# One block of a gated DeltaNet and attention model on one core: x transposed on arrival, adaLN weights in pieces of two K tiles, and the q and k projections of head 1 moved into the first stage

## The chip, the core and the metric

The program runs on one core of a Trainium2 chip. The metric is the device time of one execution in microseconds (us). A core has five engines that run side by side, each with an instruction stream of its own: TensorE (PE in the profile, with its weight loads as PEld), VectorE (DVE), ScalarE (ACT), GpSimd (POOL) and SyncE (SP), which in this program issues the DMAs. SBUF is the core's memory of 128 partitions, PSUM the eight banks into which TensorE writes.

## The reference

512 latent tokens and 256 context tokens of 2048 channels pass through one layer. All inputs are float32.

```python
mod = silu(c) @ w_ada + b_ada            # shift, scale, gate
h  = rms_norm(x, norm_w) * (1 + scale) + shift
hc = rms_norm(ctx, norm_w) * (1 + scale_c) + shift_c
p  = h @ w_in                            # q, k, v, z of 8 DeltaNet heads, gates, q, k, v, z of attention
# group A: centred conv of 5 taps and silu on q, k, v; chunks of 64;
#          delta-rule scan in both directions per head, over context and latents
# group B: 8 query heads on 2 k/v heads, rms-normed q and k, rope,
#          softmax over context and latents
y  = concat([norm(o_gdn) * silu(z_g), attn * silu(z_a)]) @ w_out
out = rms_norm(x + gate * y, final_norm_w)
```

## The kernel before, in words

The contraction over the 2048 channels runs in KT = 16 K tiles of 128. Activations lie transposed in SBUF, channels on partitions. A product of h with a weight is made in three passes: the high part of the weight with the high part of h, the high part with the low part, and the low part with the high part (`whi`, `wlo`, `hh`, `hl`; `hhL` and `hlL` hold the 512 latents, `hhC` and `hlC` the 256 context tokens). So one block of 128 weight columns is, for each K tile, three matmuls of 512 columns and, where the context is wanted too, three of 256.

**First stage (L220 to L331).** SP first loads small vectors. `ada(k)` (L245) computes shift and scale of K tile k: four pieces `wada` of 128 x 4 x 2 x 128 (each two DMAs of 256 KB in rows of 512 bytes, L253, four buffers), sixteen matmuls into four column groups of one bank (L255), a copy `part` on DVE (L258), two transposes `adat` (L261) and three small DVE operations into `md`. It runs two K tiles ahead. x and ctx are loaded into one tile `xs` by six DMAs of 1 MB in rows of 8 KB (L274), which stand in SP's queue behind the pieces of `ada(0)`. For each of the six the squares are summed on ACT (L282), the power -0.5 taken on POOL (L209), and the tile is scaled on DVE (L287). Then the loop over K tiles (L298): six transposes `xt` (L306), `hf` = `xt` times scale plus shift on DVE (L308), the high part on ACT (L311), the low part on DVE (L312), the gate columns `gps` (L315), 384 weight columns `wraw` (L321) split by ACT (L322) and POOL (L323), and the products k, v and q of head 0: `klat`, `vlat`, `qlat` with 512 columns (L327) and `cctx` with 256 for k and v (L330). In this stage a scheduler sets the order of every engine.

**Behind it** TensorE's order is the program order (`manual_schedule`, L897). `gdn_post_k`, `_q` and `_v` convolve a projected head: ACT copies PSUM into one of two buffers `craw`, DVE does four taps for k and v in two parts (L199, eight instructions) or for q in one (four). `gates(0, 1)` and `gates(1, NH)` make the decay factors, `gdn_prep(h)` the matrices of head h (its first matmul on TensorE that needs DVE is `tvh`, L620), and `gdn_scan(h)` runs the twelve dependent steps of head h: `ksh` (L717), `rh` on DVE (L731), `tsh` (L740), `vsh` on ACT (L744), `tsh` (L751), `sth` on DVE (L757). Between these dependent pieces stands filler: `feeding()` is one long list of projections (of the next heads, of attention's q, k, v and of the attention gate z), and `pull(n)` puts the next n matmul columns of that list into TensorE's order. Each scan step pulls 3900 + 2700 + 3200 columns (`F1`, `F2`, `F3`). A scan begins only when the next head is fully fed; the last one, of head 7, is run beside the preparation of attention (`attn_prep`). When the list is used up, `pull` adds nothing. The end of a head's scan shows in the trace as its last transposes `oth` (L778). Behind the last scan come attention, the z projections (L1197) and the output product (L139 to L141).

Of the kernel before, what the change touches and what calls it, by code (L numbers as in the profile page):

```python
# [68 lines left out]
def build(tc, a):  # L69
# [18 lines left out]
    hlL = hp.tile([128, KT, SEQ], F32R, name="hlL")  # L88
# [58 lines left out]
    def proj_steps(col, nm, pl, pc=None):  # L147


        for kq in range(4):  # L150
            src = w_in[kq * 512:(kq + 1) * 512, col:col + 128].rearrange("(k p) c -> p k c", p=128)
            hi, lo = wpiece(src, f"{nm}_{kq}", 128)
            for k4 in range(4):
                k = kq * 4 + k4
                for lw, rt, st, sp in ((hi[:, k4], hh, k == 0, False), (hi[:, k4], hl, False, False),
                                       (lo[:, k4], hh, False, k == KT - 1)):
                    T.matmul(pl, lhsT=lw, rhs=rt[0][:, k], start=st, stop=sp, skip_group_check=True)  # L157
                    if pc is not None:
                        T.matmul(pc, lhsT=lw, rhs=rt[1][:, k], start=st, stop=sp, skip_group_check=True)  # L159
# [1253 lines left out]
```

## Time and profile before

| | us |
|---|---|
| median of 3 runs | 1400.63 |
| lowest and highest | 1399.64 and 1403.52 |
| the profiled execution, span | 1401.1 |

For the profiled execution only the span is given; it lies inside the range of the runs. The profile has these kinds of rows. The page gives the busy time of each engine and its share, then the span in 40 slices of 35 us with a digit for the busy share, the granted clock of TensorE (`PEclk`) and the DMA rate. The timeline gives for each instruction, or run of like instructions, its start, its duration, engine, source line, result and operands, and in brackets the idle time of the engine ahead of it with what ended it. The waits view sums such idle time by engine, line and releaser. The windows view gives for a stretch the busy time of PE, PEld, DVE, ACT and POOL, then the granted clock, the share of the DMA engines and GB/s. An fp32 matmul stands in the trace as two instructions, so that its count is twice that of the program.

### The profile page before, as it was taken

How to read it: one execution, taken by the hardware profiler on the slowest of the kernel's cores; microseconds unless marked ns; L12 is line 12 of the kernel's file. 1: busy time of each engine (PE TensorE's matmuls, PEld its weight loads, DVE VectorE, ACT ScalarE, POOL GpSimd, SP SyncE). 2: the span in 40 equal slices, each digit the busy share in tenths (PEclk: the TensorE clock that was granted, in tenths of full speed). 3: DMA queues.
4: the chain of work that ended last, by engine and by line, in shares of the span. 5: the costliest groups of instructions: out<-in, count | busy, mean ns of one | idle time of the engine just before them, and what ended most of it. 6: DMA issues, size and time to landing. Idle time of an engine off the chain costs nothing.

```text
span 1401.1 us, 24994 instructions
## 1 busy us (share of the span) xinstructions
PE 1277.1 (91%) x9406; PEld 1023.1 (73%) x9406; DVE 755.5 (54%) x1650; ACT 609.2 (43%) x1509; POOL 520.5 (37%) x470
## 2 busy tenths in 40 slices
PE   3888898999999999999999999889999999999997
PEld 1455576877888787787777887767777787777785
DVE  3444685566546656476665624427676665544322
ACT  4111342445444453544545444446566664433221
POOL 1011211334253453443434444534777772011330
PEclk9999998999999999999999999999999999999998
DMA  9999632222323223232232344353545432474302
GB/s 312 280 286 282 162 71 61 59 63 57 74 66 74 62 69 73 58 83 57 82 61 65 71 121 122 90 189 99 162 137 158 133 102 59 169 231 143 94 33 100
DMA packets 264187, 163.52 MB, mean 117 GB/s; under 512 B 63042, under 2 KB 236187, under 8 KB 263043
## 3 DMA queue, kind: packets, MB, share of 16 engines
q1 hardware_dynamic: 264067, 161.93, 42.1%
q8 instruction: 74, 1.21, 0.4%
q14 instruction: 46, 0.38, 0.1%
HBM read 148.33 MB, written 13.56 MB: 116 GB/s over the span
## 4 chain that ended last, share of the span: by engine, by line
PE 53%; DVE 18%; issue 8%; DMA 8%; ACT 7%; POOL 4%; SPq 2%; POOLq 0%; ACTq 0%; DVEq 0%
PE vl L157 5%; PE zl L1197 5%; PE kl L157 3%; PE vx L159 3%; DVE cacc_v L199 2%; DVE cacc_k L199 2%; PE kvl L157 2%; DMA wada<-in_w_ada 2%; PE tsh L751 2%; PE ql L157 2%; PE po L140 2%; PE po L141 2%; PE po L139 2%; PE tsh L740 2%; PE ada L255 2%
## 5 line engine op out<-in xcount | busy, mean ns | idle before, releaser
L215 POOL TENSOR_TENSOR sdh<-sth,egl 128x256 f32<-128x256 f32 x80 | 55.5, 694 | 169.7 <-DVE sth L757 75.7
L1238 POOL TENSOR_TENSOR gacc<-graw,gacc 128x512 f32<-128x512 f32 x60 | 90.1, 1502 | 48.3 <-ACT graw L1236 35.8
L736 ACT ACTIVATE oqh<-ksh,egsw 64x128 f32<-64x128 f32 x128 | 46.4, 362 | 99.2 <-DVE rh L731 98.4
L123 POOL TENSOR_TENSOR wlo_z<-wraw_z,whi_z 128x512 fp32r<-128x512 f32 x52 | 69.7, 1342 | 52.4 <-ACT whi_z L122 52.4
L731 DVE SCALAR_TENSOR_TENSOR rh<-ksh,negeg,vtokh 64x128 f32<-64x128 f32 x176 | 61.2, 348 | 50.8 <-PE ksh L719 47.5
L1197 PE MATMUL zl<-hhL,whi_z 128*128 128x512 f32 x208 | 85.4, 411 | 0.0
L1197 PE MATMUL zl<-hhL,wlo_z 128*128 128x512 f32 x208 | 82.5, 397 | 0.1
L1197 PE MATMUL zl<-hlL,whi_z 128*128 128x512 f32 x208 | 82.5, 397 | 0.0
L757 DVE TENSOR_TENSOR sth<-sdh,tsh 128x256 f32<-128x256 f32 x80 | 33.7, 421 | 87.2 <-PE tsh L751 81.9
L140 PE MATMUL po<-wlo_wo,mh 128*128 128x512 f32 x192 | 76.8, 400 | 4.0 <-DVE wlo_wo L123 4.0
L139 PE MATMUL po<-whi_wo,mh 128*128 128x512 f32 x192 | 76.1, 399 | 3.1 <-DVE tt L215 1.6
L141 PE MATMUL po<-whi_wo,ml 128*128 128x512 f32 x192 | 76.0, 396 | 0.0
L123 DVE TENSOR_TENSOR wlo_wo<-wraw_wo,whi_wo 128x512 fp32r<-128x512 f32 x48 | 37.7, 794 | 65.7 <-ACT whi_wo L122 65.7
L199 DVE SCALAR_TENSOR_TENSOR cacc_v<-craw,cvT,cacc_v 128x512 f32<-128x512 f32 (+1 forms) x64 | 44.0, 734 | 38.9 <-ACT cacc_v L195 38.5
L1344 POOL TENSOR_TENSOR yx<-yx,tt 128x512 f32<-128x512 f32 x12 | 17.2, 1447 | 128.0 <-DVE tt L215 67.6
L816 DVE TENSOR_TENSOR ptl<-pt,pth 128x512 fp32r<-128x512 f32 x48 | 31.9, 688 | 58.4 <-ACT pth L815 58.2
L751 PE MATMUL tsh<-vsh,ktok 128*128 128x128 f32 x352 | 55.6, 281 | 3.6 <-ACT vsh L744 3.2
L122 ACT CAST whi_wo<-wraw_wo 128x512 fp32r<-128x512 f32 x48 | 29.2, 618 | 60.6 <-PE po L141 40.8
L323 POOL TENSOR_TENSOR wlo<-wraw,whi 128x384 fp32r<-128x384 f32 x16 | 16.1, 1013 | 106.1 <-ACT whi L322 106.1
L751 PEld LDWEIGHTS tsh<-vsh,ktok 128*128 128x128 f32 x352 | 47.8, 192 | 10.1 <-ACT vsh L744 4.6
L744 ACT ACTIVATE vsh<-tsh,cch 128x128 f32<-128x128 f32 x88 | 32.3, 367 | 45.7 <-PE tsh L740 44.7
L1119 ACT ACTIVATE pr<-s,mx 128x768 f32<-128x768 f32 x32 | 28.6, 898 | 53.2 <-PE zl L1197 32.7
(488 smaller groups left out, 4165.2 us busy)
## 6 DMA issues: line engine op xcount, KB each, us to landing
wada<-in_w_ada SPq DMA_DIRECT2D x128, 256.0 KB, 5.3
graw<-in_w_ada SPq DMA_DIRECT2D x64, 256.0 KB, 2.6
wraw_z<-in_w_in SPq DMA_DIRECT2D x52, 256.0 KB, 3.2
wraw_wo<-in_w_out SPq DMA_DIRECT2D x48, 256.0 KB, 3.5
wraw_q<-in_w_in SPq DMA_DIRECT2D x28, 256.0 KB, 3.1
wraw_k<-in_w_in SPq DMA_DIRECT2D x28, 256.0 KB, 2.8
wraw_v<-in_w_in SPq DMA_DIRECT2D x28, 256.0 KB, 2.8
xs<-in_x SPq DMA_DIRECT2D x4, 1024.0 KB
```

The source lines that it names most:

```text
L123: (lo_eng or G).tensor_tensor(out=lo, in0=raw, in1=hi, op=ALU.subtract)
L139: T.matmul(out, lhsT=lh, rhs=rh, start=start, stop=False, skip_group_check=True)
L140: T.matmul(out, lhsT=lh, rhs=rl, start=False, stop=False, skip_group_check=True)
L141: T.matmul(out, lhsT=ll, rhs=rh, start=False, stop=stop, skip_group_check=True)
L157: T.matmul(pl, lhsT=lw, rhs=rt[0][:, k], start=st, stop=sp, skip_group_check=True)
L199: V.scalar_tensor_tensor(out=x, in0=raw[:, i0 + j:i0 + j + m], scalar=w(j), in1=x, op0=ALU.mult, op1=ALU.add)
L215: eng.tensor_tensor(out=out, in0=x, in1=y, op=ALU.mult)
L731: V.scalar_tensor_tensor(out=r[rows], in0=ks[rows, d], scalar=gsc["negeg"][rows, gcol:gcol + 1], in1=vtok[rows, p], op0=ALU.mult, op1=ALU.add)
L736: S.activation(oq[rows, v, p - 2], ks[rows, d], AF.Copy, scale=gsc["egsw"][rows, gcol:gcol + 1])
L751: T.matmul(ts[:, d], lhsT=ktok[:, p, half], rhs=vs, start=True, stop=True, skip_group_check=True)
L1197: T.matmul(pl, lhsT=lw, rhs=rt[:, k], start=st, stop=sp, skip_group_check=True)
L1238: G.tensor_tensor(out=acc, in0=raw, in1=acc, op=ALU.add)
```

## The change

Seven things change together.

1. x and ctx come first in SP's queue, each of the six in a tile of its own. The pool `big` has five buffers of 8 KB per partition, which the x tiles and the `wada` pieces share. Each x tile is squared, scaled and transposed at once: sixteen transposes in ten groups, over four PSUM banks, whose copies into SBUF go in turn to DVE and ACT. The copies lie where the low part of h is written later.
2. K tiles come in groups of 1, 1, 2, 2, 2, 2, 2, 2, 1, 1. For a pair, `ada` loads four pieces of 128 x 4 x 2 x 256 (rows of 1 KB, 512 KB for each DMA) and multiplies 512 columns at once; for a single tile two pieces of 128 x 8 x 2 x 128 in rows of 512 bytes.
3. `first_weights` loads 640 weight columns for a K tile: q and k of heads 0 and 1 in rows of 1 KB, v of head 0 in rows of 512 bytes. `project(k)` makes five column blocks: `klat0`, `vlat0`, `klat1`, `qlat0`, `qlat1`.
4. TensorE's order is written out from the x transposes on: one piece of `ada(g + 2)` behind each column block, `gps` at the end of a K tile.
5. Behind the stage, `gdn_post_k(1)` and `gdn_post_q(1)` follow those of head 0, with three buffers `craw` in place of two.
6. The list of filler loses q and k of head 1 (24,576 and 36,864 columns, 61,440 together) and is ordered anew: v of head 1, the four k and v blocks of attention, then for each head h from 2 on k, q, v and the attention query block h - 2.
7. Some pulls grow: 16000 to 22000, 12000 and 4000 to 14000 and 6000, 3000 to 8000, and the last five of `prep` from 41000 together to 53000.

```diff
+    GROUPS = (1, 1, 2, 2, 2, 2, 2, 2, 1, 1)
...
+    es_p0.enter_context(tc.manual_schedule(engines={mybir.EngineType.PE}))
+    BIG = 5
...
+        for g, n in enumerate(GROUPS):
+            tp = banks[(t * len(GROUPS) + g) % 4](f"xt{t}_{g}")[:, :n]
...
+                T.transpose(out=tp[:, i], in_=xt_[:, c0:c0 + 128], identity=ident)
...
+            if g % 2:
+                S.copy(dst, tp)
+            else:
+                V.tensor_copy(dst, tp)
...
+        cols, rows = n * 128, 4 if n == 2 else 8
...
+                SY.dma_start(wt[:, :, s], src.rearrange("(k p) c -> p k c", p=128))
...
+                T.matmul(ada_ps[32 * q:32 * q + 32, :2 * cols], lhsT=cs[:, kk], rhs=wt[:, r].rearrange("p s c -> p (s c)"),
...
+        for c, pl, pcx in ((2, klat, cctx[:, 0]), (4, vlat, cctx[:, 1]), (3, klat1, cctx1[:, 0]),
+                           (0, qlat, None), (1, qlat1, None)):
...
+            yield
...
+    for g in range(len(GROUPS)):
+        if g + 1 < len(GROUPS):
+            group_h(g + 1)
+        ahead = ada(g + 2) if g + 2 < len(GROUPS) else iter(())
+        for i in range(GROUPS[g]):
+            for _ in project(first_k[g] + i):
+                next(ahead, None)
...
-    craw = [cvp.tile([128, 774], F32, name=f"craw{i}") for i in range(2)]
+    craw = [cvp.tile([128, 774], F32, name=f"craw{i}") for i in range(3)]
...
+    gdn_post_k(1, klat1, cctx1[:, 0])
+    gdn_post_q(1, qlat1)
...
-        yield from feed_q(1)
-        yield from feed_k(1)
         yield from feed_v(1)
-        yield from feed_kva(0)
+        for i in range(4):
+            yield from feed_kva(i)
+        fed.add("kva")
         for h in range(2, NH):
             yield from feed_k(h)
             yield from feed_q(h)
             yield from feed_v(h)
-            yield from feed_kva(h - 1) if h < 4 else feed_qa(h - 4)
-        yield from feed_kva(3)
-        fed.add("kva")
-        for h in range(4, NH):
+            yield from feed_qa(h - 2)
+        for h in range(6, NH):
             yield from feed_qa(h)
...
-    pull(16000)
+    pull(22000)
...
-    for n in (3000, 5500, 5500, 4000, 12000, 4000):
+    for n in (3000, 5500, 5500, 4000, 14000, 6000):
...
-    run(g1, 3000, 9000, 3000)
+    run(g1, 3000, 9000, 8000)
...
-    run(prep, 4000, 24000, 4000, 5000, 4000)
+    run(prep, 5000, 30000, 5000, 7000, 6000)
```

**TensorE in the first stage.** Before, around one K tile; `ada_501` belongs to a K tile two further on, and the projection of this K tile starts at `klat`:

```order
L306 MATMUL xt_0_694<-cmain,xs 128x128 x4
L306 MATMUL xt_1_700<-cmain,xs 128x128 x2
L255 MATMUL ada_501<-wada_12_523,cs 32x256 x4
L261 MATMUL adat_532<-cmain,part_530 128x128 x2
L327 MATMUL klat_265<-hhL,whi_3_558 128x512
L330 MATMUL cctx_268<-hhC,whi_3_558 128x256
L327 MATMUL klat_265<-hlL,whi_3_558 128x512
L330 MATMUL cctx_268<-hlC,whi_3_558 128x256
L327 MATMUL klat_265<-hhL,wlo_3_559 128x512
```

In the change, at its first K tile (`klat_512` is k of head 0, `vlat_513` v of head 0):

```order
L383 MATMUL klat_512<-hhL,w0h_464 128x512
L385 MATMUL cctx_517<-hhC,w0h_464 128x256
L383 MATMUL klat_512<-hL_475,w0h_464 128x512
L385 MATMUL cctx_517<-hC_476,w0h_464 128x256
L383 MATMUL klat_512<-hhL,w0l_465 128x512
L385 MATMUL cctx_517<-hhC,w0l_465 128x256
L319 MATMUL ada_541<-wada_0_542,cs 32x512 x4
L383 MATMUL vlat_513<-hhL,w0h_464 128x512
L385 MATMUL cctx_517<-hhC,w0h_464 128x256
```

The transposes of x have left the K tile, and a piece of `ada`, now 512 columns wide, stands between two column blocks instead of ahead of all of them.

**TensorE in the last scan, of head 7.** Before, from the eleventh step on, with z blocks of attention (`zal1a`, `zal2a`) as filler:

```order
L717 MATMUL ksh_9229<-sth_9_9836,kq_7804 128x128
L719 MATMUL ksh_9229<-sth_9_9836,kq_7804 128x128
L157 MATMUL zal1a<-hlL,whi_z1a_9808 128x512
L157 MATMUL zal1a<-hhL,wlo_z1a_9809 128x512
L157 MATMUL zal2a<-hhL,whi_z2a_9861 128x512
L157 MATMUL zal2a<-hlL,whi_z2a_9861 128x512
L157 MATMUL zal2a<-hhL,wlo_z2a_9862 128x512
...
L820 MATMUL qtp_9871<-cmain,ktok_1555 128x128 x4
L740 MATMUL tsh_10_9880<-rh_10_9845,UU_2029 128x128
```

In the change, from the fifth step into the sixth (`ktp` and `kps` belong to the preparation of attention):

```order
L827 MATMUL tsh_4_9597<-rh_4_9583,UU_2182 128x128
L838 MATMUL tsh_4_9597<-vsh_4_9599,ktok_1653 128x128 x2
L847 MATMUL oh_9582<-vnh_4_9601,IB_1661 128x128
L907 MATMUL ktp_9608<-cmain,ktok_1652 128x128 x4
L804 MATMUL ksh_9362<-sth_4_9605,kq_7952 128x128
L806 MATMUL ksh_9362<-sth_4_9605,kq_7952 128x128
L827 MATMUL tsh_5_9624<-rh_5_9615,UU_2182 128x128
L907 MATMUL kps_9630<-cmain,kvch_9571 128x128 x2
L838 MATMUL tsh_5_9624<-vsh_5_9626,ktok_1653 128x128 x2
L847 MATMUL oh_9582<-vnh_5_9628,IB_1661 128x128
L804 MATMUL ksh_9362<-sth_5_9643,kq_7952 128x128
L806 MATMUL ksh_9362<-sth_5_9643,kq_7952 128x128
```

No filler row stands between the dependent matmuls any more: the list is used up in the fourth step.

**VectorE behind the first stage.** Before, around the point where head 0's preparation first reads `gqh` into `IB`; `cacc_q_1697` is q of head 1:

```order
L553 TENSOR_TENSOR grh_1677<-grh_1677,cmain 128x384 x2
L199 SCALAR_TENSOR_TENSOR cacc_q_1697<-craw_1460,cvT,cacc_q_1697 128x512
L532 TENSOR_SCALAR skh_1762<-ssh_1680 128x2
L123 TENSOR_TENSOR wlo_k_3_1908<-wraw_k_3_1905,whi_k_3_1907 128x512
L199 SCALAR_TENSOR_TENSOR cacc_q_1697<-craw_1460,cvT,cacc_q_1697 128x512
L539 RECIPROCAL rk2h_1769<-skh_1762 128x6
L215 TENSOR_TENSOR IB_1563<-gqh_1793,grh_1677 64x4x64
```

In the change, at the same point, with the end of the taps of k of head 1 (`cacc_k_1623`) in the first two rows:

```order
L214 SCALAR_TENSOR_TENSOR cacc_k_1623<-craw_1526,cvT,cacc_k_1623 128x512
L214 SCALAR_TENSOR_TENSOR cacc_k_1623<-craw_1526,cvT,cacc_k_1623 128x256
L492 SCALAR_TENSOR_TENSOR ug<-ug,w_g 128x84 x2
L493 SCALAR_TENSOR_TENSOR ug<-ug,s_g 128x84
L227 SCALAR_TENSOR_TENSOR kq_1619<-craw_1526,cacc_k_1623 128x4x64 x2
L227 SCALAR_TENSOR_TENSOR kc_1620<-craw_1526,cacc_k_1623 128x2x64 x2
L619 TENSOR_SCALAR skh_1894<-ssh_1810 128x2
L494 TENSOR_SCALAR ug<-ug 128x84
L626 RECIPROCAL rk2h_1901<-skh_1894 128x6
L495 SCALAR_TENSOR_TENSOR zg<-zg,ug 128x84
L630 TENSOR_TENSOR cch_1905<-beta,rk2h_1901 128x12
L230 TENSOR_TENSOR IB_1660<-gqh_1923,grh_1807 64x4x64
```

Eight taps of k of head 1 now stand ahead of that point, and the taps of its v stand ahead of the transposes `NTh` that follow some rows further on; before, both stood behind `NTh`.

More of the change, by code (lines that the diff above doesn't have):

```diff
@@ L87, in build @@
     hhL = hp.tile([128, KT, SEQ], F32R, name="hhL")
-    hlL = hp.tile([128, KT, SEQ], F32R, name="hlL")
+    GROUPS = (1, 1, 2, 2, 2, 2, 2, 2, 1, 1)
+    first_k = [sum(GROUPS[:g]) for g in range(len(GROUPS))]
+    place = [(g, i) for g, n in enumerate(GROUPS) for i in range(n)]
     es_hc = ExitStack()
@@ L91, in build, with low_tile, hl, hpass @@
     hhC = hpc.tile([128, KT, CTX], F32R, name="hhC")
-    hlC = hpc.tile([128, KT, CTX], F32R, name="hlC")
-    hh, hl = (hhL, hhC), (hlL, hlC)
+    hh = (hhL, hhC)
+    xts, hls = {}, {}
+    lows = ((hp, SEQ, "L"), (hpc, CTX, "C"))
+    def low_tile(m, g, dtype, nm):
+        pool_, n, s = lows[m]
+        return pool_.tile([128, GROUPS[g], n], dtype, tag=f"l{s}{g}", bufs=1, name=f"{nm}{s}{g}")
+    def hl(m, k):
+        g, i = place[k]
+        return hls[m, g][:, i]
+    def hpass(k, hi, lo):
+        return (hi, [t[:, k] for t in hh]), (hi, [hl(m, k) for m in range(2)]), (lo, [t[:, k] for t in hh])
     cmain = cst.tile([128, 416], F32, name="cmain")
@@ L290, in build, with group_h @@
+    def group_h(g):
+        for i in range(GROUPS[g]):
+            first_weights(first_k[g] + i)
+        make_h(g)
+    for _ in ada(0):
+        pass
     SY.dma_start(wg, w_in[:, COL_G:COL_G + 32].rearrange("(k p) c -> p k c", p=128))
+    group_h(0)
+    for _ in ada(1):
+        pass
     klat = PP.tile([128, SEQ], F32, tag="pl", name="klat0")
+    vlat = PP.tile([128, SEQ], F32, tag="pl", name="vlat0")
     qlat = stile([128, SEQ], "qlat0", "o")
-    vlat = PP.tile([128, SEQ], F32, tag="pl", name="vlat0")
+    klat1 = stile([128, SEQ], "klat1", "k")
@@ L295, in build @@
+    qlat1 = stile([128, SEQ], "qlat1", "s")
     cctx = PC.tile([128, 2, CTX], F32, tag="pc", name="cctx0")
[L296 to L331 removed]
@@ L334, in build @@
+    cctx1 = btile([128, 2, CTX], "cctx1")
+    gps = cctx1[:, 1]
+    for g in range(len(GROUPS)):
+        if g + 1 < len(GROUPS):
+            group_h(g + 1)
+        ahead = ada(g + 2) if g + 2 < len(GROUPS) else iter(())
+        for i in range(GROUPS[g]):
+            for _ in project(first_k[g] + i):
+                next(ahead, None)
+        for _ in ahead:
+            pass
     es0.close()
```

196 lines of the change are left out of this document (107 added, 89 removed).

## The prediction

> **What bounds the kernel now.** I read the page first: the span and the busy shares, then the slices.
>
> ```profile
> span 1401.1 us, 24994 instructions
> PE 1277.1 (91%) x9406; PEld 1023.1 (73%) x9406; DVE 755.5 (54%) x1650; ACT 609.2 (43%) x1509; POOL 520.5 (37%) x470
> PE   3888898999999999999999999889999999999997
> DMA  9999632222323223232232344353545432474302
> GB/s 312 280 286 282 162 71 61 59 63 57 74 66 74 62 69 73 58 83 57 82 61 65 71 121 122 90 189 99 162 137 158 133 102 59 169 231 143 94 33 100
> ```
>
> TensorE is busy 91% of the time, so a gain has to come out of its idle 9%. Each digit covers 35 us: PE is at 3 and 8 in the first slices, where the DMA engines stand at 9. So the first stage is the one place that is bound by transfers; behind it TensorE binds. Next the windows and TensorE's timeline of one K tile.
>
> ```profile
> 10.00:20.00 10.00, 3.92 (x26) 0.94 (x26) 1.37 (x7) 3.25 (x5) 0.56 (x1) 1.00 1.06 392
> 40.00:150.00 110.00, 96.06 (x819) 56.84 (x821) 47.33 (x108) 19.63 (x41) 13.16 (x13) 1.00 1.09 285
> 1230.00:1240.00 10.00, 10.00 (x44) 8.07 (x43) 2.67 (x4) 1.86 (x3) 0.00 (x0) 1.00 1.00 374
> 82.10 1.07 PE L255 MATMUL ada<-wada,cs 128*32 128x256 f32 x16
> 82.99 0.59 PE L315 MATMUL gps<-hf,wg 128*32 128x256 f32 x2
> 83.88 0.64 PE L255 MATMUL ada<-wada,cs 128*32 128x256 f32 x8 [0.29 <-DMA wada<-in_w_ada]
> 84.87 0.88 PE L306 MATMUL xt<-cmain,xs 128*128 128x128 f32 x6
> 86.93 0.44 PE L261 MATMUL adat<-cmain,part 128*128 128x128 f32 x2 [0.54 <-DVE part L258]
> 87.12 0.48 PE L327 MATMUL klat<-hhL,whi 128*128 128x512 f32 x1
> 90.00 0.40 PE L327 MATMUL qlat<-hhL,wlo 128*128 128x512 f32 x1
> 162.77 0.50 PE L327 MATMUL qlat<-hhL,wlo 128*128 128x512 f32 x1
> ```
>
> From 40 to 150 us the queue carries 285 GB/s with its engines full (share above 1), in rows of 512 bytes; rows of 8 KB (x, first window) went at 392 and rows of 2 KB (output weights, third window) at 374. In a K tile the three projections take 87.12 to 90.32, 3.2 us; the other 5.0 us ahead of `klat` hold adaLN, gates, transposes and waits of 0.29 and 0.54. The stage's last projection starts at 162.77; I call 162.8 its end.
>
> **Part 1: the first stage, +4 us.** The pitch of the moved work:
>
> ```profile
> 182.63 0.39 PE L157 MATMUL kl<-hhL,whi_k 128*128 128x512 f32 x1
> 182.86 0.28 PE L159 MATMUL kx<-hhC,whi_k 128*128 128x256 f32 x1
> 182.98 0.40 PE L157 MATMUL kl<-hlL,whi_k 128*128 128x512 f32 x1
> ```
>
> By the starts, 512 columns take 0.23 to 0.24 us and 256 columns 0.12. `q` of a head is 48 x 0.235 = 11.3 us, `k` 48 x 0.352 = 16.9, so 28.2 us of TensorE work move into the stage. A K tile's five blocks are 15 x 0.235 + 9 x 0.117 = 4.6 us.
>
> x on arrival: ACT sets its end.
>
> ```profile
> 9.06 1.19 SPq L274 DMA_DIRECT2D xs<-in_ctx  x2
> 16.50 1.06 ACT L282 ACTIVATE junk<-xs 128x1024 bf16<-128x1024 f32 x1 [10.25 <-DMA xs<-in_ctx]
> 17.46 0.19 ACT L282 ACTIVATION_READ_ACCUMULATOR junk<-xs 128x1 f32 x1
> L122 ACT CAST whi_wo<-wraw_wo 128x512 fp32r<-128x512 f32 x48 | 29.2, 618 | 60.6 <-PE po L141 40.8
> ```
>
> x is issued at 9.06 now, behind the eight DMAs of `ada(0)`; ahead of them it goes some 5 us sooner, so the first tile is there about 10 us. Squares are 2.5 us a tile, 15 for six; ACT's half of the copies is 1024 columns a tile, at 0.62 for 512 some 1.6 us with the overhead of five instructions, 10 for six. End at 35 to 37; then `ada(0)`, `md`, `hf`, its high and low part, about 5 us: the first projection starts near 42. The six moved DMAs delay `ada(0)` by 6.3 MB / 392 = 16 us, which lies beside that ACT work; and 0.88 x 16 = 14 us of transposes leave the K tiles for this stretch, where TensorE had little to do.
>
> Then the transfers. Up to the end of `ada(3)` SP brings 6.3 MB of x, 4.5 MB in rows of 512 bytes (single tiles and `wg`), 1.3 MB of projection weights and 8.4 MB in rows of 1 KB. No row of the trace shows 1 KB; the bounds are 285 and 374, and I take 340, just above the middle of the two. That gives 4 + 16 + 16 + 4 + 25 = 65 us, and a few more where pieces wait for the x tiles to leave the five shared buffers: the first two K tiles are paced by DMA, to about 70. In the written order a piece that hasn't landed holds the column blocks behind it on TensorE; nobody else waits for these then, as the next tiles' h comes from the same pieces. Behind them TensorE binds: fourteen tiles x 4.6 = 64; `ada` is 0.9 us for 8 matmuls of 256 columns in four column groups (82.10 to 82.99), so 3.6 for a pair's 16 of 512, 4 pairs and 2 singles 18; `gps` 0.6 a tile with its three together, 8; `adat` 4; waits 2 to 3, since a piece of `ada` now runs between blocks and `part` has a whole block to hide behind. 70 + 97 = **167**, +4. ACT and POOL split 640 weight columns a tile in place of 384: POOL's 13 splits cost 13.2 of 110 us in the window from 40 to 150 and ACT is busy 19.6 there, so both stay far from full, and I cost this at nothing; if the low part came late, a block would stand for 0.7 us. All 45.4 MB take to about 146 us at these rates, so the queue is done first. With 374 for rows of 1 KB and nothing lost at the start, the stage ends at 157; with 285, near 178.
>
> The Trainium skill, "DMA: Bandwidth & Descriptors", section Specifications, puts the minimum for line rate at 512 B, by which longer rows would gain nothing; the windows of 285 and 374 disagree with it between 512 bytes and 2 KB. Its section "Why small descriptors are slow" gives a fixed overhead of about 3 cycles a packet beside 32-byte beats, by which I estimate 285 x (32/35) / (16/19) = 309 for 1 KB, and the stage would end some 6 us later than I say.
>
> **Part 2: from there to the end of head 0's scan, +18 us.** The ends of the scans, and a window behind the stage:
>
> ```profile
> 344.70 0.66 PE L778 MATMUL oth<-cmain,oqh 128*128 128x128 f32 x4
> 855.79 0.60 PE L778 MATMUL oth<-cmain,oqh 128*128 128x128 f32 x4
> 160.00:300.00 140.00, 125.80 (x976) 104.12 (x975) 95.92 (x282) 59.10 (x162) 30.48 (x30) 0.94 0.28 65
> 920.78 0.38 PE L760 MATMUL oh<-vnh,IB 128*128 128x128 f32 x2
> 926.00 1.20 PE L778 MATMUL oth<-cmain,oqh 128*128 128x128 f32 x4 [0.64 <-ACT oqh L774]
> ```
>
> 162.8 to 344.7 is 181.9 us. Counted in the two orders, 256,512 columns of filler stand there before and 305,152 in the change (four k and v blocks of attention come early, the pulls grow): 48,640 x 0.235 / 512 = +22.3. TensorE is idle for 140 - 125.8 = 14.2 us of the window from 160 to 300. The larger pulls lie there, ahead of the steps of the gates and of head 0's preparation, so each us of filler can cover a us of wait; but VectorE gets more to do in the same stretch (first rival). I credit 4 us, about a third. Bounds: +9, if all the waits went, and +30, if VectorE holds TensorE (first rival).
>
> **Part 3: heads 1 to 6, -12 us.** 344.7 to 855.8 is 511.1 us. The orders hold 135,168, 134,656, three times 122,880 and 113,664 columns before and five times 122,880 and 113,664 after: 24,064 fewer, 11.0 us; TensorE is full there (nines), so they count whole, and a wait of the first of these scans may go with them, 1 us.
>
> **Part 4: the last scan, -15 us.** 855.8 to 926.0 is 70.2 us with 97,280 columns; the change leaves 11,264 there, 39.5 us fewer, and its steps five to twelve are bare. What a bare step costs is a chain of these rows:
>
> ```profile
> 917.32 0.38 PE L717 MATMUL ksh<-sth,kq 128*128 128x128 f32 x2
> 917.96 0.72 DVE L731 SCALAR_TENSOR_TENSOR rh<-ksh,negeg,vtokh 64x128 f32<-64x128 f32 x2 [1.92 <-PE ksh L719]
> 912.04 0.48 PE L740 MATMUL tsh<-rh,UU 128*128 128x128 f32 x2
> 912.85 0.37 ACT L744 ACTIVATE vsh<-tsh,cch 128x128 f32<-128x128 f32 x1
> 897.15 0.61 PE L751 MATMUL tsh<-vsh,ktok 128*128 128x128 f32 x4
> 914.46 1.06 PE L751 MATMUL tsh<-vsh,ktok 128*128 128x128 f32 x4
> 883.53 0.42 DVE L757 TENSOR_TENSOR sth<-sdh,tsh 128x256 f32<-128x256 f32 x1
> ```
>
> 917.32 to 918.68 for the first two, 912.04 to 913.22 for the next two, 0.61 for `tsh` at the full clock (1.06 at half), 0.42 + 0.1 for `sth`: 3.7 us and two hand-overs of 0.1, so 3.9, or 4.3 at the lower clock. Eight steps: 31 to 34. Ahead of them the 11,264 columns and a step, 9; the epilogue 5.2 as now (920.78, the last `oh`, to 926.0). Attention's preparation stands in the same order and can hold a step:
>
> ```profile
> 910.00:920.00 10.00, 8.42 (x39) 7.30 (x40) 3.21 (x6) 3.02 (x7) 1.87 (x3) 0.83 0.29 79
> 911.58 0.63 PE L820 MATMUL qtp<-cmain,ktok 128*128 128x128 f32 x4 [3.21 <-DVE ktok L812]
> ```
>
> One such wait of 3.2 us under filler; I put 5 to 8 for the bare steps. In all 51 to 57, I take 55. Bounds: no such waits, 46; every step still 6 us, 68.
>
> The Trainium skill, "TensorE: Matmul & The Clock Gate", Part 1, halves the clock after an idle window of about 3.4 us; here it fell behind the 3.21 us wait (1.06 against 0.61), which fits, and shorter gaps inside a bare step would by that rule keep 3.9.
>
> **The rest, 0 +- 3.** Behind 926.0 stand 475.1 us whose code changes only in where the low part of h lies.
>
> **Sum:** 4 + 18 - 12 - 15 = -5, so 1401.1 - 5 = **1396**. The profiled span is 0.5 above the median, inside the runs' range; I add nothing. About 0.3% (4 us) is what a measurement of this kernel can tell from no change. Adding the ends of the parts in squares (9, 7, 2, 5, 3) gives +-13 at the widest, so the likeliest case's own range is 1385 to 1408.
>
> **Rivals.**
>
> *VectorE takes over behind the first stage (slower).* Its rows there:
>
> ```profile
> 190.00:200.00 10.00, 8.93 (x65) 7.27 (x64) 9.89 (x28) 4.45 (x11) 3.70 (x2) 1.00 0.20 52
> 183.08 5.54 DVE L199 SCALAR_TENSOR_TENSOR cacc_v<-craw,cvT,cacc_v 128x512 f32<-128x512 f32 x8
> 200.05 0.41 PE L620 MATMUL tvh<-cmain,vv 128*128 128x128 f32 x2 [1.12 <-DVE grh L215]
> ```
>
> VectorE is full from 190 to 200, and TensorE waits for it at `tvh`, 37 us behind the stage's end. Two convolutions of 5.54 (k and v of head 1) now stand ahead in its order, so the same point comes about 47 us behind; TensorE's own stream with the longer pulls reaches it after 40. It decides where VectorE is more than 3 us late, since a few us hide in the pulls: up to 9 us of wait and 3 more at a half-rate clock, so part 2 is +30 and the time **1408**. Against it: some DVE rows there are small and fall in gaps. Chance 0.2.
>
> *Rows of 1 KB gain nothing (the change does not do what it says).* The stage ends near 178: 1396 + 11 = **1407**. The 374 of the 2 KB rows speaks against it. The rule on line rate above would have it so. Chance 0.08.
>
> *The last scan gains nothing* where attention's preparation, not the steps, sets the pace: 68 in place of 55, **1409**. The single 3.21 us wait speaks for it, VectorE's 3.21 busy us of 10 in that window against. Chance 0.07.
>
> *Transfers as fast as 2 KB rows, and more of the waits covered:* stage end 157, **1386**. Chance 0.17.
>
> **Chances.** The forecast case keeps 0.48. Faster than 1396.4 are about half of it (0.26) and the last rival; same (1396.4 to 1404.8) 0.17 of it and 0.12 of the edges of the slower cases; slower the rest. So faster 0.43, same 0.30, slower 0.27. The range takes in the fast rival's lower side and the three slow ones: 1382 to 1411.
>
> **What would show it.** Rate near 340 GB/s from 70 to 140 us, and a stage end at 165 to 170; TensorE's waits at `tvh` of 2 us or less; `oth` of head 0 at 360 to 375, then 81 to 88 us a head; the last segment 51 to 57 with steps of about 4 us. I am wrong if `tvh` waits 9 us, if the stage ends past 175, or if a bare step takes 6.

## The result and the profile after

| | us |
|---|---|
| the change, median of 4 runs | 1422.18 (1418.51 to 1424.78) |
| before, median of 4 runs | 1401.49 (1399.64 to 1403.52) |
| ratio, 95% interval | 1.0142 (1.012 to 1.0165) |
| the profiled execution of the change | 1418.51, span 1416.3 |

The change makes the kernel slower by 1.4%; the forecast was 1396. The profiled execution was the fastest of the four, so what follows accounts for 15.2 us between the two spans (1401.1 and 1416.3); the other 5 us to the ratio of the medians are scatter between executions and are not assigned to anything.

The page of the changed kernel, its span, engine shares and slices of 35 us:

```profile
span 1416.3 us, 24550 instructions
PE 1281.7 (90%) x9214; PEld 1021.2 (72%) x9214; DVE 767.8 (54%) x1666; ACT 614.5 (43%) x1531; POOL 517.3 (37%) x465
PE   4789979999999999999999999769989899999997
PEclk8999999999999999999999999879999999999999
DMA  8999412332232323223232344323555442474312
GB/s 263 328 346 290 120 53 59 93 67 66 78 66 59 72 69 75 62 57 84 58 77 61 81 90 121 96 86 113 150 148 161 129 112 60 163 236 143 92 37 95
```

The rate in the second and third slice is up from 280 and 286 to 328 and 346 GB/s, and PE is at 9 in the fourth and fifth slice; but a 7 stands in the sixth, right behind the first stage, and a 7 and a 6 have come in at slices 26 and 27, where the last scan lies, with the clock at 8 and 7. The same five stretches of both kernels in the windows view (start and end, length, busy time of PE, PEld, DVE, ACT and POOL, granted clock, DMA share, GB/s), before first: the first stage, from there to the end of head 0's scan (its `oth`), heads 1 to 6, the last scan, the rest. The mark of 162.8 is the start of the last projection before; that matmul ends at 163.3. In the change and the runs on it, the stage's end is the end of its last matmuls, those of the gate columns.

```profile
0.00:162.80 162.80, 123.65 (x984) 70.56 (x984) 69.90 (x162) 41.25 (x79) 26.17 (x40) 1.00 1.02 279
162.80:344.70 181.90, 165.07 (x1487) 137.93 (x1486) 118.64 (x328) 80.82 (x230) 50.21 (x48) 0.95 0.26 61
344.70:855.80 511.10, 485.47 (x4473) 408.09 (x4472) 291.78 (x734) 237.57 (x662) 212.13 (x204) 1.00 0.31 74
855.80:926.00 70.20, 63.68 (x337) 52.13 (x336) 26.78 (x53) 32.94 (x97) 34.96 (x33) 0.98 0.34 96
926.00:1401.10 475.10, 439.21 (x2132) 354.37 (x2132) 248.38 (x373) 216.59 (x444) 197.08 (x145) 0.98 0.43 131
```

The change:

```profile
0.00:180.00 180.00, 148.71 (x930) 89.39 (x930) 78.90 (x172) 53.08 (x112) 34.25 (x42) 0.95 0.87 267
180.00:381.20 201.20, 183.99 (x1620) 155.93 (x1619) 118.23 (x334) 85.64 (x238) 56.87 (x54) 0.97 0.27 65
381.20:886.20 505.00, 477.17 (x4369) 395.84 (x4368) 297.56 (x734) 236.08 (x661) 211.32 (x205) 1.00 0.31 75
886.20:945.10 58.90, 34.56 (x170) 26.97 (x168) 24.32 (x53) 23.63 (x80) 17.65 (x19) 0.75 0.19 60
945.10:1416.30 471.20, 437.23 (x2132) 353.09 (x2132) 248.78 (x373) 216.05 (x443) 197.25 (x145) 0.99 0.43 129
```

Length less busy PE is TensorE's idle. It goes from 39.2 to 31.3 us in the first stage, 16.8 to 17.2 up to head 0's scan, 25.6 to 27.8 in heads 1 to 6, 6.5 to 24.3 in the last scan and 35.9 to 34.0 in the rest. So the first stage took in 25.1 us of busy time and used up only 7.9 us of idle: it got 17.2 us longer, half a microsecond of which comes from the two marks. The last scan has 29.1 us less to do and is only 11.3 shorter.

TensorE's timeline in the first stage of the change: one pair of K tiles, from one `gps` (on the bank of `cctx1`) to the one two tiles on, and the end of the stage.

```profile
94.70 0.63 PE L388 MATMUL cctx<-hf,wg 128*32 128x256 f32 x6
96.50 1.06 PE L319 MATMUL ada<-wada,cs 128*32 128x512 f32 x8
98.74 1.06 PE L319 MATMUL ada<-wada,cs 128*32 128x512 f32 x8
106.48 0.60 PE L327 MATMUL adat<-cmain,part 128*128 128x128 f32 x4
110.53 0.63 PE L388 MATMUL cctx<-hf,wg 128*32 128x256 f32 x6
174.04 0.63 PE L388 MATMUL cctx<-hf,wg 128*32 128x256 f32 x6
179.37 0.63 PE L388 MATMUL cctx<-hf,wg 128*32 128x256 f32 x6
```

No row has a bracket: TensorE waits for nothing there. The pair takes 15.8 us, a tile without adaLN 5.3. The largest group of TensorE's waits in this stage (engine, line, what was waited for: us in total, times, longest):

```profile
PE ada L319 <- DMA wada<-in_w_ada: 10.5, 9, 3.2
```

The last of these nine ends at 87 us. From there on the stage is TensorE's own work. Its first projection, with the last row of `ada` ahead of it:

```profile
45.48 1.93 PE L319 MATMUL ada<-wada,cs 128*32 128x256 f32 x16 [3.15 <-DMA wada<-in_w_ada]
48.30 0.78 PE L383 MATMUL klat<-hhL,w0h 128*128 128x512 f32 x1
```

VectorE finishes the low part of h of the first tile at 43.97 (its row for `hC` starts at 43.55 and takes 0.42). In the written order all of `ada(1)` stands ahead of the first projection, and its second piece lands late, so the projections start 4.3 us later than h would let them.

### The profile page after: what moved, and what is told of

The parts are those of the page before. It is cut to its first block, busy times and chain, and to the rows that moved or that the text cites. A ratio compares the mean times of both kernels' runs of the same rounds, so it can differ in the third digit from the quotient of the medians.

```text
span 1416.3 us, 24550 instructions
## 1 busy us (share of the span) xinstructions
PE 1281.7 (90%) x9214; PEld 1021.2 (72%) x9214; DVE 767.8 (54%) x1666; ACT 614.5 (43%) x1531; POOL 517.3 (37%) x465
## 4 chain that ended last, share of the span: by engine, by line
PE 52%; DVE 19%; issue 9%; ACT 7%; DMA 6%; POOL 5%; SPq 1%; POOLq 0%; DVEq 0%; ACTq 0%
PE vl L172 5%; PE zl L1281 4%; PE kl L172 3%; PE vx L174 3%; DVE cacc_v L214 3%; PE kvl L172 3%; DMA wada<-in_w_ada 2%; DVE cacc_k L214 2%; PE po L155 2%; PE tsh L838 2%; PE po L156 2%; PE po L154 2%; DVE rh L818 2%; DVE tmh L694 2%; PE ql L172 2%
## 5 line engine op out<-in xcount | busy, mean ns | idle before, releaser
L1281 PE MATMUL zl<-hL,whi_z 128*128 128x512 f32 x208 | 82.4, 396 | 0.0
L353 POOL TENSOR_TENSOR w0l<-w0r,w0h 128x640 fp32r<-128x640 f32 x16 | 24.9, 1561 | 107.4 <-PE cctx L388 56.4
L214 DVE SCALAR_TENSOR_TENSOR cacc_v<-craw,cvT,cacc_v 128x256 f32<-128x256 f32 (+1 forms) x64 | 41.6, 696 | 33.9 <-ACT cacc_v L210 33.5
L827 PE MATMUL tsh<-rh,UU 128*128 128x128 f32 x176 | 38.4, 301 | 21.8 <-DVE rh L818 21.7
L827 PEld LDWEIGHTS tsh<-rh,UU 128*128 128x128 f32 x176 | 28.4, 194 | 33.7 <-issue 15.2
```

The lines of the kernel that those rows point to most:

```text
L214: V.scalar_tensor_tensor(out=x, in0=raw[:, i0 + j:i0 + j + m], scalar=w(j), in1=x, op0=ALU.mult, op1=ALU.add)
L827: T.matmul(ts[:, 2], lhsT=UU[:, w], rhs=r, start=True, stop=True, skip_group_check=True)
L1281: T.matmul(pl, lhsT=lw, rhs=rt, start=k == 0 and m == 0, stop=k == KT - 1 and m == 2, skip_group_check=True)
```

## The experiments

A first set of four takes the change apart at the places that the account names: the moved blocks, the row size, the empty list, the pulls.

**three.** The moved blocks back in the list, the rest of the change kept:

```diff
-        for c, pl, pcx in ((2, klat, cctx[:, 0]), (4, vlat, cctx[:, 1]), (3, klat1, cctx1[:, 0]),
-                           (0, qlat, None), (1, qlat1, None)):
+        for c, pl, pcx in ((1, klat, cctx[:, 0]), (2, vlat, cctx[:, 1]), (0, qlat, None)):
...
-    gdn_post_k(1, klat1, cctx1[:, 0])
-    gdn_post_q(1, qlat1)
...
+        yield from feed_q(1)
+        yield from feed_k(1)
         yield from feed_v(1)
         for i in range(4):
             yield from feed_kva(i)
```

> The change with q and k of head 1 put back at the front of the filler list, so that the first stage makes three column blocks again (384 weight columns a K tile in rows of 512 bytes); all else stays. In the changed kernel the first stage ends at 180.0 and the span is 1416.3. Theory A (the stage is TensorE's own work from about 89 us on, so the moved blocks lengthen it nearly one for one, and the shorter list leaves the last scan bare): the stage ends at 150 to 155, the segment of the last scan has its filler back, span 1395 to 1403. Theory B (a late start and the transfers set the end of the stage, whatever is projected in it): the stage still ends past 168, span 1410 or more.

Measured: 1418.83 us, ratio to before 1.0113 (1.0079 to 1.0146). Windows of three, the first stage and the stretch behind it:

```profile
0.00:154.60 154.60, 118.99 (x783) 68.21 (x786) 68.20 (x172) 48.30 (x109) 25.71 (x42) 0.94 0.97 296
154.60:379.30 224.70, 214.16 (x1770) 181.26 (x1769) 120.34 (x334) 91.50 (x249) 68.35 (x62) 0.97 0.28 69
```

Its largest wait in the first stage:

```profile
PE ada L319 <- DMA wada<-in_w_ada: 13.6, 16, 1.5
```

The windows are cut at the end of the last projection, 154.6; the gate columns behind it end at 155.2, against 180.0 in the change. On the stage theory A holds within 0.2 us: the 28.2 us of moved blocks cost 24.8 there. On the span it misses by 15: the next stretch takes 224.7 us, longer than in the change and full of filler (10.5 us idle). That pointed at the list's order: head 1's scan may not start before head 2 is fed, and here head 1's q and k and the four attention blocks all stand ahead of that.

**row512.** The pieces of the pairs loaded in rows of 512 bytes:

```diff
-                SY.dma_start(wt[:, :, s], src.rearrange("(k p) c -> p k c", p=128))
+                for c0 in range(0, cols, 128):
+                    SY.dma_start(wt[:, :, s, c0:c0 + 128], src[:, c0:c0 + 128].rearrange("(k p) c -> p k c", p=128))
```

> The change with every piece for a pair of K tiles loaded by DMAs of 128 columns, in rows of 512 bytes (256 KB each) instead of 1 KB; nothing else differs. Theory A (TensorE binds the stage from 89 us on): the rate between 40 and 70 us falls from 335 to about 285 GB/s, the end of the stage moves by at most 4 us, span at most 1421. Theory B (transfers set the end): 25.2 MB at 285 instead of 335 GB/s is 13 us, the stage ends at 190 to 194, span about 1428.

Measured: 1426.03, ratio 1.0164 (1.0125 to 1.0203); the stage ends at 187.0, 7.0 later, between the two expectations. The waits for pieces grow from 10.5 to 13.5 us and the last of over 1 us ends at 92 us, so transfers bind a little longer than in the change, but not to the end.

**nza5.** Two z blocks more in the list: `NZA = 3` becomes `NZA = 5`.

> The change with five z blocks of attention in the filler list instead of three (the two taken from the z projections behind the scans, so the work is the same). Theory A (the last scan's idle is only a list that ran out; TensorE idles 24 of 62 us there and runs at a clock of 0.76): the two blocks' 22.6 us go into that idle, the segment of the last scan grows by 0 to 8 us, the z projections shorten by 22, span 1398 to 1404. Rival (attention's preparation paces that scan, and filler only pushes it out): the segment grows by 20, span 1413 or more.

Measured: 1413.52, ratio 1.0085 (1.0038 to 1.0131), span 1410.4. The last scan takes 68.2, the part behind it 456.8 instead of 471.2. Both theories miss: 5.9 us of span gained of the expected 12 to 18, with the segment of the last scan 9.3 longer, beyond the 0 to 8 of the one and short of the 20 of the other.

**pulls_before.** The pulls of before in the change:

```diff
-    pull(22000)
+    pull(16000)
...
-    for n in (3000, 5500, 5500, 4000, 14000, 6000):
+    for n in (3000, 5500, 5500, 4000, 12000, 4000):
...
-    run(g1, 3000, 9000, 8000)
+    run(g1, 3000, 9000, 3000)
...
-    run(prep, 5000, 30000, 5000, 7000, 6000)
+    run(prep, 4000, 24000, 4000, 5000, 4000)
```

> The change with the pulls of before behind the first stage (16000, 12000 and 4000, 3000, and 4000, 24000, 4000, 5000, 4000): 27,000 columns, 12.4 us, move from ahead of head 0's scan to the end of the list, that is into the last scan. Theory A (those pulls hid little): the segment from the stage's end to the end of head 0's scan falls from 201 to about 189, the last scan takes the columns into its idle, span 1404 to 1408. Rival (the longer pulls cover waits for VectorE, whose order has got longer): the waits come back, that segment falls by 4 or less, span 1413 or more.

Measured: 1426.01, ratio 1.0164 (1.0134 to 1.0193), span 1424.0. The segment grew from 201.2 to 207.1 with idle 22.7: shorter pulls are worse, as the rival has it (more so: it gave a segment shorter by up to 4). The columns did not even leave the segment, since they had to be fed before head 1's scan in any case.

The second set separates the list's order from the moved blocks.

**kva_spread.** The change with one attention block behind each head, as before:

```diff
-        for i in range(4):
-            yield from feed_kva(i)
-        fed.add("kva")
+        yield from feed_kva(0)
         for h in range(2, NH):
...
-            yield from feed_qa(h - 2)
-        for h in range(6, NH):
+            yield from feed_kva(h - 1) if h < 4 else feed_qa(h - 4)
+        yield from feed_kva(3)
+        fed.add("kva")
+        for h in range(4, NH):
```

> The change with the order of the filler list as before: one k or v block of attention behind each head, in place of all four ahead of head 2; the first stage, the pulls and everything else as in the change. Theory A (what makes the segment up to the end of head 0's scan long is the list: the scan of head 1 may not begin before head 2 is fed, and the four early blocks, 147,456 columns, stand ahead of head 2): now the pulls bind, 277,600 columns instead of 305,152, so that segment falls by 12 us from 201 to about 189, and by 6 more if the wait of a context block for its copy (6.0 us) goes; the later heads take 82 to 83 us with 117,600 columns each, the last scan gets about 70,000 columns and takes 66 to 70 us: span 1394 to 1402. Rival (VectorE's longer order behind the stage sets it): that segment stays above 196, span 1408 or more.

**stage_only.** `three` with that list and the pulls of before, so the old kernel with the new first stage alone.

> The kernel before with the rewritten first stage alone: three column blocks (q and k of head 1 stay in the filler list), the list's order and the pulls as before, three buffers craw. Theory A (the rewritten stage gains by itself, the moved blocks and the list's order lose it again): the stage ends at 154.4 as in the run three, the rest takes 1238 us as before: span 1391 to 1395. Rival (the new stage leaves something behind that costs later, in the order of VectorE or the place of the low part of h): rest above 1246, span 1400 or more.

**stage_pulls.** `stage_only` with the longer pulls.

> As stage_only, with the longer pulls of the change. 21,600 more columns, 9.9 us, stand ahead of the end of head 0's scan and 21,600 fewer behind it. If the waits behind the stage are covered by them (some 17 us of idle there before), the segment grows by less than 7 us and the span is 1384 to 1390; if not, it grows by 10 and the span is that of stage_only, 1391 to 1396.

**spread_nza5.** `kva_spread` with `NZA = 5`.

> kva_spread with five z blocks in the list instead of three: the last scan gets about 119,000 columns, as much as it can pull. If what idle it has left in kva_spread is only an empty list, the segment of the last scan grows by 14 to 20 us and the part behind it shortens by 18 to 22: span 2 to 6 below kva_spread. If not, the same span within 2 us.

Measured:

| | us | ratio to before (95%) | stage's end | to head 0's `oth` | heads 1 to 6 | last scan | span |
|---|---|---|---|---|---|---|---|
| kva_spread | 1424.12 | 1.0150 (1.0126 to 1.0174) | 179.3 | 197.1 | 501.4 | 72.8 | 1421.7 |
| stage_only | 1397.93 | 0.9973 (0.9959 to 0.9987) | 154.8 | 186.4 | 510.7 | 70.2 | 1398.0 |
| stage_pulls | 1393.50 | 0.9941 (0.9919 to 0.9964) | 155.6 | 184.9 | 505.2 | 70.1 | 1389.5 |
| spread_nza5 | 1426.06 | 1.0174 (1.0149 to 1.0199) | 177.8 | 198.3 | 501.4 | 76.8 | 1423.6 |

`kva_spread` is a miss for theory A: the segment up to head 0's `oth` shrank by 4, not 12 to 18, and the span rose. The rival's two numbers are met; that VectorE is what holds the segment is tested below. The wait of a context block for its copy stays too (5.98 us). `spread_nza5` gains nothing over it. `stage_only` came out 3 us above its range, 4.6 us faster than before by the medians; with the longer pulls it is 9.0 us faster, the best of all: there the segment did not grow at all (186.4 to 184.9), so the longer pulls cover waits, as the first of the two expectations has it. Four of the spans make a square:

| span, us | attention blocks spread | attention blocks first |
|---|---|---|
| three column blocks in the first stage | 1389.5 (stage_pulls) | 1417.9 (three) |
| five | 1421.7 (kva_spread) | 1416.3 (the change) |

Either edit alone costs about 30 us (28.4 and 32.2); the two together cost 27. VectorE's transposes `NTh` and the first step `ksh` of head 0's scan, in stage_pulls (stage's end 155.6):

```profile
193.93 1.57 DVE L670 STREAM_TRANSPOSE NTh<-grh 32x192 f32<-32x192 f32 x4
244.88 0.38 PE L805 MATMUL ksh<-sth,kc 128*128 128x256 f32 x1
```

and in kva_spread (179.3):

```profile
229.36 1.57 DVE L674 STREAM_TRANSPOSE NTh<-grh 32x192 f32<-32x192 f32 x4
277.92 0.70 PE L809 MATMUL ksh<-sth,kc 128*128 128x256 f32 x2
```

VectorE comes to `NTh` 38.4 us behind the stage's end in the one and 50.1 in the other, and the scan starts 89.3 and 98.6 us behind it.

The third set tests that reading, the last scan again, and what the new stage gains by.

**late_post.** `kva_spread` with the taps of head 1's q and k moved behind the first six pieces of head 0's preparation; ACT copies the banks out at once:

```diff
-    gdn_post_k(1, klat1, cctx1[:, 0])
-    gdn_post_q(1, qlat1)
...
+    for nm, pl_, pc_ in (("k1", klat1, cctx1[:, 0]), ("q1", qlat1, None)):
...
+        early[nm] = conv_in(pl_, pc_, raw_)
...
         pull(n)
         next(prep, None)
+    gdn_post_k(1, klat1, cctx1[:, 0])
+    gdn_post_q(1, qlat1)
     run(g1, 3000, 9000, 8000)
```

> kva_spread with the taps of k and q of head 1 put behind the first six pieces of head 0's preparation: their PSUM banks are copied out by ACT at once, into two buffers of their own, and VectorE makes the taps later. In kva_spread VectorE reaches the transposes NTh 50.1 us behind the stage's end and the first scan starts at 94.9; in stage_pulls, where q and k of head 1 are projected later, 38.9 and 86.2. Theory A (the taps of head 1 ahead in VectorE's order cost that segment its 11.6 us): NTh at 40 to 43, first scan at 86 to 90, the end of head 0's scan at 186 to 190 instead of 197, span 7 to 12 below kva_spread's 1421.7. Rival (it is the copies of the five banks, or the list): NTh past 46, span within 4 of it.

Measured: 1420.51, ratio 1.0117 (1.0084 to 1.0150), span 1418.7. VectorE's `NTh`, and the first matmul `pxah` behind it:

```profile
220.19 1.57 DVE L681 STREAM_TRANSPOSE NTh<-grh 32x192 f32<-32x192 f32 x4
255.17 0.27 PE L734 MATMUL pxah<-DTh,grh 32*32 32x32 f32 x2 [5.19 <-DVE DTh L726]
```

The stage ends at 180.1. `NTh` is back at 40.1 us behind it, as theory A has it; but the taps now delay VectorE's `DTh`, for which TensorE waits 5.19 us (2.29 in kva_spread), and the segment takes 191.1 us, half of the way back from 197.1 to 184.9. The span falls by 3.0, where theory A gave 7 to 12 and the rival at most 4. The edit moves ACT's copies as well as the taps, and TensorE's largest wait of the segment goes with them: context matmuls for ACT's `craw`, 6.4 us in kva_spread, 0.8 here. So the place of head 1's taps and copies together costs the segment 6.0 us; the two weren't separated. Of the other 6.2, most is a wait that both runs have and stage_pulls has not, at the first step of head 1's scan. In kva_spread, VectorE's eight taps of the next k (that of head 2) and TensorE's wait for the last copies of `UU`:

```profile
351.22 5.43 DVE L214 SCALAR_TENSOR_TENSOR cacc_k<-craw,cvT,cacc_k 128x512 f32<-128x512 f32 x8 [0.29 <-ACT cacc_k L210]
357.19 0.76 PE L827 MATMUL tsh<-vtokh,UU 128*128 128x128 f32 x2 [4.83 <-DVE UU L773]
```

The taps stand between the copies of `UU` in VectorE's order.

**nza5_even.** `nza5` with the last scan's pulls halved: `pull(n if h + 1 < NH else n // 2)`.

> nza5 with the pulls of the last scan halved, so that its some 60,000 columns reach over all twelve steps instead of the first six. Theory A (the two added blocks gained only 5 us because they stood where TensorE was full, and the last steps stayed bare): idle of TensorE in the segment of the last scan falls from 18.3 to 6 to 11, the segment from 68 to 56 to 62, span 1398 to 1404. Rival (the steps wait for attention's preparation, which is as late as before): the segment stays above 65, span 1407 or more.

Measured: 1421.14, ratio 1.0133 (1.0106 to 1.0161), span 1418.0. The window of the last scan in nza5:

```profile
885.40:953.60 68.20, 49.89 (x265) 40.20 (x263) 26.02 (x53) 28.78 (x90) 27.86 (x27) 0.88 0.31 90
```

and in nza5_even:

```profile
887.20:952.30 65.10, 50.65 (x261) 39.55 (x260) 25.65 (x54) 28.76 (x93) 24.94 (x26) 0.92 0.25 73
```

A miss for theory A, and the rival's numbers are met: nearly the same busy time, idle 14.4 instead of 18.3, and 9 us more behind the scan (465.7 instead of 456.8), where TensorE has 7.7 us more to do. The wait for attention's preparation (`qtp` for VectorE's `ktok`) is 4.8 us, as in nza5 and in the change (4.7 in both). Filling the last scan better does not get back what the empty list costs.

**stage_512.** `stage_pulls` with the row edit of `row512`.

> stage_pulls (three column blocks) with the adaLN pieces in rows of 512 bytes. In row512, with five blocks, the stage ended 6.4 us later than in the change. Theory A (with three blocks the stage is bound by transfers, so row size counts in full there): 25.2 MB at about 287 instead of 335 GB/s, the stage ends at 162 to 168 instead of 155, span 1396 to 1402, and the gain of the rewritten stage is the row size. Rival (x on arrival is the gain): the stage ends at 158 or sooner, span 1393 or less.

Measured: 1411.19, ratio 1.0055 (1.0034 to 1.0075). The window from 90 to 140 us in stage_pulls:

```profile
90.00:140.00 50.00, 45.61 (x310) 24.80 (x310) 21.42 (x51) 10.96 (x24) 8.04 (x8) 1.00 1.10 322
```

and in stage_512:

```profile
90.00:140.00 50.00, 38.36 (x247) 19.44 (x246) 18.58 (x45) 9.43 (x20) 5.99 (x6) 1.00 1.16 290
```

The stage ends at 170.9, 15.4 later than with rows of 1 KB and 7.6 later than before the change (163.3). So with three blocks the rows are more than the whole gain of the new stage; the rest of it (x first, pieces of 1 MB, the written order) costs some 8 us against the old one at the same row size. Which of these costs them was not tried.

## Why the prediction was wrong

| | before | forecast | measured |
|---|---|---|---|
| first stage | 162.8 | 167 | 180.0 |
| to the end of head 0's scan | 181.9 | 200 | 201.2 |
| heads 1 to 6 | 511.1 | 499 | 505.0 |
| last scan | 70.2 | 55 | 58.9 |
| rest | 475.1 | 475 | 471.2 |

**Part 1, the first stage, is the step that failed.** I put +4 for it and measured +17.2; an end past 175 was among the prediction's own signs of being wrong. The rate was about right: 335 GB/s in the window from 40 to 70 us, where 340 was taken for rows of 1 KB. The first two tiles, paced by DMA, were to end at 70 and ended at 75.6, and the pacing lasted on to 87. The term that I left at "a few more" is one cause: SP's queue stood while the x tiles left the five shared buffers, and the transfers ran at 0.67 to 0.84 of the engines from 15 to 30 us. SP's largest group of waits up to 45 us and one of these windows:

```profile
SPq L315 <- PE xt L295: 10.1, 4, 4.1
20.00:25.00 5.00, 2.83 (x16) 1.53 (x14) 3.62 (x8) 4.28 (x13) 1.06 (x2) 0.92 0.67 246
```

By the shares of three such windows (0.70, 0.67, 0.84) I estimate 4 us of lost transfer time, of the 5.6 by which the two tiles were late; no run with more buffers tests it. `wg`, which the sum has in rows of 512 bytes, has rows of 128 (32 columns): 233 GB/s from 30 to 35 us, with the engines full. That the first projection started at 48.3 instead of 42 need not have mattered by itself, as pieces still came late behind it. The other 7.4 us are in the fourteen tiles, priced at 97 and measured at 104.4: 3.3 of waits for pieces in the first pair, where 2 to 3 were allowed for all; and a tile 5.3 instead of 5.2, a pair 15.8 instead of 14.6, since each `ada` piece takes about 1.0 instead of 0.9 (1.06 busy) and each change between `ada` and a block costs a tenth or two.

What the moved blocks themselves cost was priced rightly: fourteen sixteenths of 28.2 us, 24.7, stand in the sum behind the DMA-paced tiles, and three against the change shows 24.8. So without them the sum's terms make the rewritten stage some 20 us shorter than the old one, and it was 8 shorter (155.2 against 163.3). The idle 39.2 us of the old stage could not pay for the blocks: in three, 22.4 of 35.6 us of idle lie in the first 50 us, and the waits for pieces behind are 1.5 us or less each.

The rival on row size was mispriced. Its 178 for the stage's end is 11 later than 167, while the sum holds only 8.4 MB in rows of 1 KB up to `ada(3)`, 4.8 us more at 285 instead of 340; row512 shows 7.0 in the change, and 15.4 with three blocks (stage_512). The stage ended at 180.0 though the rows did gain.

**Part 2** was +18 and came out +19.3, for mixed reasons. The first rival, VectorE, was priced at 47 us to `tvh` and 9 us of wait. `tvh` came at 49.1, but TensorE's wait there was 2.3. Another wait had held TensorE before it: the context matmuls of the first attention block waited 6.04 us for ACT's copy of the block ahead of them, v of head 1, out of the one bank that context blocks have. The rows of the change, `NTh`, `tvh` and that wait:

```profile
229.40 1.57 DVE L674 STREAM_TRANSPOSE NTh<-grh 32x192 f32<-32x192 f32 x4
229.12 0.66 PE L707 MATMUL tvh<-cmain,vv 128*128 128x128 f32 x2 [2.34 <-DVE grh L230]
209.38 0.58 PE L174 MATMUL kvx<-hhC,whi_kv 128*128 128x256 f32 x1 [6.04 <-ACT craw L199]
```

I had not seen that wait; what `tvh` would have waited without it was not tried. That the number came out near +18 is luck: the idle did not shrink by the 4 us credited (16.8 to 17.2), and busy time grew by 18.9 where 22.3 was counted. Nor had I weighed the rule that a scan waits until the next head is fed, though its columns are in the count of 305,152: it is what makes the early attention blocks cost 39.2 us in this segment with three blocks (three against stage_pulls, 224.1 against 184.9). With five blocks the same order costs 4.1 there (201.2 against 197.1).

**Part 3** was -12 and came out -6.1. The mechanism is right for two heads, the size was taken for whole: heads 1 and 2 lost 12,288 and 11,776 columns, 5.6 and 5.4 us, and got 4.1 and 3.6 us shorter, and head 6 got 1.6 longer, which no run explains.

**Part 4** was 55 and came out 58.9. Bare steps and the end, timeline of the change in the last scan (the first two rows lie ahead of the others), and two windows:

```profile
905.40 0.80 PE L804 MATMUL ksh<-sth,kq 128*128 128x128 f32 x2 [0.39 <-DVE sth L844]
911.40 0.76 PE L804 MATMUL ksh<-sth,kq 128*128 128x128 f32 x2
918.15 0.66 PE L804 MATMUL ksh<-sth,kq 128*128 128x128 f32 x2 [0.21 <-DVE sth L844]
922.59 0.49 PE L804 MATMUL ksh<-sth,kq 128*128 128x128 f32 x2
926.92 0.49 PE L804 MATMUL ksh<-sth,kq 128*128 128x128 f32 x2 [0.39 <-DVE sth L844]
932.34 1.09 PE L907 MATMUL qtp<-cmain,ktok 128*128 128x128 f32 x4 [4.71 <-DVE ktok L899]
934.75 1.22 PE L838 MATMUL tsh<-vsh,ktok 128*128 128x128 f32 x4 [0.90 <-ACT vnh L834]
945.07 1.35 PE L865 MATMUL oth<-cmain,oqh 128*128 128x128 f32 x4 [4.31 <-ACT oqh L861]
900.00:905.00 5.00, 3.39 (x24) 2.62 (x23) 1.89 (x5) 2.56 (x9) 0.62 (x1) 0.99 0.00 0
905.00:910.00 5.00, 3.35 (x13) 2.67 (x13) 1.97 (x6) 2.11 (x9) 1.27 (x2) 0.50 0.24 78
```

The bare steps, from one `ksh` to the next, took 4.4, 4.3, 6.0, 6.8, 4.4, 4.3 and 9.6 us, where I took 3.9 to 4.3; a step of 6 was another sign of being wrong. The 9.6 hold one wait for attention's preparation of 4.7; I had put 5 to 8 for all such waits. The 4.31 at `oth` is no miss: from the last `oh` (939.97) it took 5.1, as priced (5.2).

The steps of 6.0 and 6.8 ran at half the clock, and there I weighed the clock wrongly. I took it that short gaps keep the full rate. The granted clock falls from 0.99 to 0.50 at 905 us and stays there to 918, and no wait of TensorE in this segment ahead of that is longer than 1.07 us; the wait of 2.21 us for VectorE's `rh`, in the step of 6.8, comes later. Behind the wait of 4.71, `tsh` is at 1.22 against 0.71 in the steps before. The idle window of about 3.4 us of the Trainium skill ("TensorE: Matmul & The Clock Gate", Part 1) fits that wait and not the fall at 905. What set off that fall was not tried.

**The rest** was 3.9 us shorter, which I had at 0 with 3 either way; no run explains it.

**The chances.** Slower by over 0.3% had 0.27, all of it through single mechanisms of 11 to 13 us, and the range ended at 1411. The forecast added its terms as if what leaves the list were gained later. The square shows the opposite: with the list spread, moving the blocks costs 32.2 us of span. 23.8 are the stage, 12.2 the stretch up to head 0's scan. Heads 1 to 6 have 14.1 us less to do and return only 3.8, because their idle grows by 10.2, from 28.1 in stage_pulls:

```profile
340.50:845.70 505.20, 477.11 (x4427) 399.97 (x4426) 294.03 (x734) 234.76 (x658) 207.18 (x202) 1.00 0.30 73
```

to 38.3 in kva_spread:

```profile
376.40:877.80 501.40, 463.06 (x4300) 386.76 (x4299) 284.75 (x724) 229.64 (x648) 199.73 (x196) 0.98 0.29 70
```

With TensorE 91% busy I took filler for work that is better done early; it is also what covers the other engines' chains behind the stage, and there it was missing. Shown are the three sizes: 24.8 in the stage, 39.2 for the list's order with three blocks, 6.0 for the place of head 1's taps and copies. What holds the scans of heads 4 and 5 in kva_spread, which take 88.3 and 86.7 us there and 85.1 and 85.0 in stage_pulls, was not tried and stays open.

## What to carry to other kernels

Filler that stands between dependent steps is cover. Before moving it into an earlier stage, ask how much of that stage's idle is of a kind that it can fill (waits of the same stretch, not a start that no work can precede), and who waits uncovered later. Where a list of filler also decides when a dependent stage may begin, count the columns up to each such point, not only the total. And an edit that bundles a gain with a loss is taken apart best by a square of runs: here the rewritten stage with the longer pulls, without the moved blocks and with the old order of the list, is 0.6% faster than before.

## What the hardware showed

With pieces in rows of 1 KB the queue moved 342 GB/s from 50 to 85 us and 343 from 90 to 120 (stage_pulls), with the same pieces in rows of 512 bytes 291 and 290 (stage_512), its engines full in all four (share above 1). From 120 to 140 us, where stage_pulls loads pieces of single tiles and both have rows of 512 bytes, both read 289; that is why its window from 90 to 140 shows 322. Those pieces of single tiles come in DMAs of 512 KB, the pieces of stage_512 in DMAs of 256 KB, so the row and not the size of the DMA goes with the rate. The window from 50 to 85 us of stage_pulls:

```profile
50.00:85.00 35.00, 23.77 (x159) 10.36 (x157) 9.98 (x28) 5.65 (x12) 3.96 (x4) 1.00 1.11 342
```

and of stage_512:

```profile
50.00:85.00 35.00, 25.33 (x136) 11.40 (x128) 7.79 (x22) 4.29 (x10) 2.95 (x3) 0.81 1.15 291
```

That is a step of 18%, larger than the 8% that I worked out from the fixed overhead in the Trainium skill ("DMA: Bandwidth & Descriptors", "Why small descriptors are slow"), and its line-rate minimum of 512 B (Specifications) does not hold on this queue. For rows of 8 KB the prediction's 392 mixes x with the last pieces of `ada(0)`: in the change, where x is issued ahead of all pieces, the window from 10 to 15 us reads 421.
